# A decoder layer with 32 experts: ten chunks of expert weights ahead of the first expert, and another order of the x2 updates

## Chip, cores and metric

One core of a Trainium2 chip runs the kernel as one program. The metric is the device time in microseconds of an execution; 1505.49 us is the median of three (1504.41 to 1506.1).

## What is computed

The reference is one decoder layer on 256 tokens of 2048 columns in float32. `w_ada` times silu(c) gives six rows of 2048 (shift, scale and gate of both halves). The first half is a norm with shift and scale, one input projection, two token mixers (a gated linear recurrence, `hgrn`, and latent attention, `mla`) and one output projection, gated by `g1`. The second is a mixture of 32 experts of which each token takes two.

```python
h = _modulate(_rmsnorm(x, norm1_g[l]), sh1, sc1)
proj = h @ w_in[l]
...
mix = jnp.concatenate([o_a, o_b], axis=-1) @ w_out[l]
x = x + g1[:, None, :] * mix
h2 = _modulate(_rmsnorm(x, norm2_g[l]), sh2, sc2)
y = _hier_moe(h2, w_group[l], b_group[l], w_router[l], b_router[l],
              w_gate[l], w_up[l], w_down[l])
x = x + g2[:, None, :] * y
```

Inside `_hier_moe`: the softmax over four groups, the best group, the best two of its eight experts, and for each expert `(silu(xb @ w_gate) * (xb @ w_up)) @ w_down`, weighted and summed per token.

## The kernel before, in words

All weights come through one ring of buffers of [128, 4096] float32, 2048 KB a chunk, in one order (`items`): `w_ada`, `w_in`, the low-rank weights of the attention, `w_out`, then for each expert four chunks `gu` (gate and up) and two chunks `dn` (down). `ring_fill` (L156) issues the next load on SP's queue whenever a slot is free and `ring_done` (L172) frees a slot. Four slots are there from the start (`ringA`); two more (`ringB`, `RING2`) come when the temporaries of the mixers are closed behind `w_out(0, 1)` (`close_temps`, L794); and one (`ringC`) when the split buffers are closed behind the last dense product. So at most seven chunks of experts are in SBUF when the router ends. SP also loads x again, in tiles of 512 columns, for the residual (L556).

`dense` (L377) splits each 128 x 512 piece of weights in two parts: ScalarE rounds it (L385), VectorE takes the difference (L386), and TensorE makes three products with the split input (L400 to L402 here). `w_out(half, j)` runs the output projection for block j of 512 columns: half 0 over the attention's half of the rows into `mix0`, half 1 over the recurrence's. Behind half 1, three pairs of VectorE instructions (one for each 128 tokens) make the new residual (L549 to L551):

```python
V.tensor_add(m[:, t], m[:, t], ps[t])
V.tensor_mul(m[:, t], m[:, t], gate[:, 512 * j:512 * j + 512])
V.tensor_add(x2[j][:, t], x2[j][:, t], m[:, t])
```

`x2_ready` (L588) takes the squares of block j, transposes it on TensorE (`px2T`, L599), copies the transpose (L601, L603) and adds its part of the router's logits (`plog`, L607). The text calls block j of x2 a tile. Between the dense products TensorE computes the rows of `w_ada` (`pada`, L265); the last 24 of these matmuls belong to the gate of the second half, and `ada_end` adds them to a row `brows` (L274). `gate_rows` (L912) spreads that row over the partitions.

The router (L837 to L903) is a chain of small VectorE steps from the logits `lg` (L842) to the ranks of the tokens within their experts. `dispatch` (L919 to L944) gathers the tokens of four experts by matmuls with one-hot rows (`pgat`, L933) and evacuates with shift and scale (`XT`, L938). The expert loop then runs `pgu` (L1003), `hidden` and `down` (L979), and `combine` (L956).

Within an engine the instructions run in the order that the scheduler of the tile framework chose when the program was built; the Python text gives only priorities. SP issues its loads in the order of the text, and a load that waits holds all behind it.

Of the kernel before, what the change touches and what calls it, by code (L numbers as in the profile page):

```python
# [9 lines left out]
F32 = mybir.dt.float32  # L10
# [9 lines left out]
# buffers: weight ring, 4 KB tiles that live long, 4 and 2 KB temporaries, splits, more ring later  # L20
RING, NARENA, NTEMP, NSPLIT, RING2 = 4, 14, (8, 6), 4, 2
# rows of w_ada for the gates and the second modulation: chunks behind each step of the products
SPREAD = (1, 4, 7, 5, 5, 2, 0, 0, 0, 2, 1, 1, 0)
EARLY = {28: 1}
HEAD = 2  # expert chunks loaded ahead of the last of these rows
AHEAD = 3  # steps of the first dispatch ahead of the first expert
# [19 lines left out]
def tile_hybrid_layer(ctx, tc, A, out):  # L46
# [56 lines left out]
    # ---------------------------------------------------------------- weight stream  # L103
# [92 lines left out]
    # ---------------------------------------------------------------- start: x, tables  # L196
# [18 lines left out]
    # silu(c), by channel and as a row on every partition  # L215
# [14 lines left out]
    rows = cpool.tile([P, 512], F32, name="rows")  # L230
# [5 lines left out]
    def adt_chunk(i):  # L236
        """Two tiles of 128 columns of w_ada, transposed, times silu(c)."""
# [32 lines left out]
    def ada_end(b):  # L270
        if b in ("g1", "g2"):
            brow = brows[:, ("g1", "g2").index(b)]
            for j in range(4):
                V.tensor_add(brow[32 * j:32 * j + 1], brow[32 * j:32 * j + 1], acc[b][32 * j:32 * j + 1])  # L274
# [5 lines left out]
        else:  # L280
            S.activation(rows, acc[b], AF.Copy)
# [10 lines left out]
    def norm1():  # L292
        """x * rsqrt(mean(x^2) + eps)"""
# [871 lines left out]
```

## Time and profile before

| | |
|---|---|
| runs | 1504.41, 1505.49, 1506.1 us |
| profiled execution, span | 1503.6 us |
| PE, VectorE (DVE), ScalarE (ACT) busy | 75%, 39%, 23% |
| bytes moved, mean rate | 575.61 MB, 383 GB/s |
| rate in slices 17 to 39 of 40 | 428 to 431 GB/s |
| loads of expert chunks | 128 `gu` and 64 `dn`, 2048 KB each |

The page of the profile knows no time of the profiled execution but its span. Its other parts are read so: a group of instructions gives busy time, mean, and the idle time in front of it with what ended that; a window gives each engine's busy time in a stretch, PE's granted clock (1.00 is 2.4 GHz) and the DMA's share and rate; the timeline gives single instructions, or runs of like ones, with their start.

### The profile page before, as it was taken

How to read it: one execution, taken by the hardware profiler on the slowest of the kernel's cores; microseconds unless marked ns; L12 is line 12 of the kernel's file. 1: busy time of each engine (PE TensorE's matmuls, PEld its weight loads, DVE VectorE, ACT ScalarE, POOL GpSimd, SP SyncE). 2: the span in 40 equal slices, each digit the busy share in tenths (PEclk: the TensorE clock that was granted, in tenths of full speed). 3: DMA queues.
4: the chain of work that ended last, by engine and by line, in shares of the span. 5: the costliest groups of instructions: out<-in, count | busy, mean ns of one | idle time of the engine just before them, and what ended most of it. 6: DMA issues, size and time to landing. Idle time of an engine off the chain costs nothing. (4 is left out here: it accounts for less than half of the span.)

```text
span 1503.6 us, 22669 instructions
## 1 busy us (share of the span) xinstructions
PE 1123.6 (75%) x9813; PEld 686.8 (46%) x9813; DVE 592.3 (39%) x1192; ACT 340.5 (23%) x705; POOL 5.0 (0%) x9
## 2 busy tenths in 40 slices
PE   3799999979999989776667667657667657566555
PEld 1688887637568756333323323323423423333222
DVE  6789998759765552220121121113112112112112
ACT  4564446526435432100100100100100100000000
POOL 0000000000000000000000000000000000000000
PEclk9999999989999999878887888879978888889777
DMA  9788796877979798999999999999999999999995
GB/s 382 314 320 324 284 363 244 332 283 314 367 285 382 295 374 333 429 429 431 430 431 430 429 429 430 430 431 431 430 430 429 430 430 431 431 429 428 431 431 228
DMA packets 43423, 575.61 MB, mean 383 GB/s; under 512 B 4778, under 2 KB 5034, under 8 KB 8376
## 3 DMA queue, kind: packets, MB, share of 16 engines
q1 hardware_dynamic: 41776, 570.56, 91.2%
q10 hardware_dynamic: 1544, 3.56, 0.6%
q8 instruction: 79, 1.29, 0.3%
q14 instruction: 24, 0.20, 0.0%
HBM read 572.00 MB, written 2.11 MB: 382 GB/s over the span
## 5 line engine op out<-in xcount | busy, mean ns | idle before, releaser
L1003 PE MATMUL pgu<-wch,XT 128*32 128x256 f32 x4096 | 314.4, 461 | 188.5 <-DMA wch<-in_w_gu_dram 188.4
L1003 PEld LDWEIGHTS pgu<-wch,XT 128*32 128x32 f32 x4096 | 140.5, 127 | 353.7 <-DMA wch<-in_w_gu_dram 245.1
L979 PE MATMUL py<-wch,hT 128*32 128x256 f32 x2048 | 170.3, 490 | 80.3 <-DMA wch<-in_w_down_dram 73.5
L983 DVE TENSOR_TENSOR Y<-py,gate 32x256 f32<-32x256 f32 x256 | 107.6, 420 | 222.2 <-PE py L979 219.4
L968 DVE TENSOR_TENSOR hid<-sgu,pgu 128x128 f32<-128x128 f32 x32 | 9.2, 288 | 456.2 <-ACT sgu L966 456.2
L386 DVE TENSOR_TENSOR split<-wch,split 128x512 fp32r<-128x512 f32 (+2 forms) x248 | 160.2, 668 | 69.6 <-ACT split L385 68.4
L385 ACT ACTIVATE split<-wch 128x512 fp32r<-128x512 f32 (+2 forms) x248 | 148.1, 615 | 148.5 <-PE pacc L402 99.8
L979 PEld LDWEIGHTS py<-wch,hT 128*32 128x32 f32 x2048 | 80.1, 134 | 158.4 <-issue 63.1
L966 ACT ACTIVATE sgu<-pgu 128x128 f32<-128x128 f32 x32 | 8.9, 278 | 604.4 <-PE pgu L1003 604.4
L938 ACT ACTIVATE XT<-pgat,sh,a 128x128 f32<-128x128 f32 x128 | 48.2, 457 | 219.3 <-PE pgat L933 219.2
L401 PE MATMUL pacc<-split,hhi 128*128 128x512 f32 (+1 forms) x192 | 74.3, 387 | 2.3 <-DVE split L386 2.2
L393 PE MATMUL pacc<-hhi,split 128*128 128x256 f32 x256 | 72.7, 285 | 1.2 <-ACT split L385 1.1
L395 PE MATMUL pacc<-hhi,split 128*128 128x256 f32 x256 | 72.2, 285 | 1.7 <-DVE split L386 1.7
L402 PE MATMUL pacc<-split,hlo 128*128 128x512 f32 (+1 forms) x192 | 73.2, 382 | 0.0
L400 PE MATMUL pacc<-split,hhi 128*128 128x512 f32 (+1 forms) x192 | 71.1, 385 | 2.7 <-ACT split L385 2.7
L394 PE MATMUL pacc<-hlo,split 128*128 128x256 f32 x256 | 72.7, 285 | 0.5 <-DVE hlo L357 0.5
L243 DVE SCALAR_TENSOR_TENSOR wch<-wch,gate 128x2048 f32<-128x2048 f32 x32 | 72.8, 2285 | 0.0
L956 PE MATMUL pcmb<-Y,pwt 128*128 128x512 f32 x128 | 61.2, 622 | 15.5 <-DVE Y L983 15.5
L265 PE MATMUL pada<-wch,ca 128*1 128x512 f32 x512 | 69.9, 608 | 3.8 <-DVE pada L260 3.8
L933 PEld LDWEIGHTS pgat<-ohr,x 128*128 128x128 f32 x512 | 63.3, 205 | 10.4 <-issue 9.4
L933 PE MATMUL pgat<-ohr,x 128*128 128x128 f32 x512 | 66.7, 291 | 0.7 <-DVE sm L900 0.7
L400 PE MATMUL pacc<-split,mhi 128*128 128x512 f32 x128 | 51.0, 400 | 0.0
(301 smaller groups left out, 1187.7 us busy)
## 6 DMA issues: line engine op xcount, KB each, us to landing
wch<-in_w_gu_dram SPq DMA_DIRECT2D x128, 2048.0 KB, 31.1
wch<-in_w_down_dram SPq DMA_DIRECT2D x64, 2048.0 KB, 31.1
wch<-in_w_ada_dram SPq DMA_DIRECT2D x32, 2048.0 KB, 9.6
wch<-in_w_ada_t_dram SPq DMA_DIRECT2D x16, 2048.0 KB, 9.5
wch<-in_w_in_dram SPq DMA_DIRECT2D x16, 2048.0 KB, 9.3
wch<-in_w_out_dram SPq DMA_DIRECT2D x8, 2048.0 KB, 9.6
wch<-in_w_in_dram SPq DMA_DIRECT2D x4, 1664.0 KB, 7.5
x<-in_x_dram SPq DMA_DIRECT2D x8, 512.0 KB, 10.7
```

Source lines behind the costliest of these rows:

```text
L243: V.scalar_tensor_tensor(wk, wk, 1.0, gate, op0=OP.mult, op1=OP.mult, accum_out=r[:, k:k + 1])
L385: S.activation(s[:, 0, :ncol], w, AF.Copy)
L386: V.tensor_sub(s[:, 1, :ncol], w, s[:, 0, :ncol])
L393: PE.matmul(o, s[:, 0, c], hi, start=first and h % 2 == 0, stop=False, skip_group_check=True)
L394: PE.matmul(o, s[:, 0, c], lo, start=False, stop=False, skip_group_check=True)
L400: PE.matmul(o, hi[:, c], s[:, 0, :ncol], start=first, stop=False)
L401: PE.matmul(o, hi[:, c], s[:, 1, :ncol], start=False, stop=False)
L402: PE.matmul(o, lo[:, c], s[:, 0, :ncol], start=False, stop=stop)
L933: PE.matmul(ps[:, 128 * i:128 * i + 128], x2[kt // 4][:, t, 128 * (kt % 4):128 * (kt % 4) + 128], ohr[:, t], start=t == 0, stop=t == 1)
L979: PE.matmul(py[32 * j:32 * j + 32, :256], H["T"][:, 32 * kt:32 * kt + 32], w[:, 1024 * kt + 256 * j:1024 * kt + 256 * j + 256], start=kt = ...
L983: V.tensor_mul(Y[q][r:r + 32, 256 * j:256 * j + 256], py[32 * j:32 * j + 32, :256], gate[32 * j:32 * j + 32, c:c + 256])
L1003: PE.matmul(gu[32 * j:32 * j + 32, :256], XT[G4][kt // 8][:, kt % 8, 32 * e4:32 * e4 + 32], w[:, 1024 * i + 256 * j:1024 * i + 256 * j + 2 ...
```

## The change

It does these things:

- `RING2` is 3 instead of 2, so eight ring slots can hold chunks. The space comes from the constants (`cst` keeps 448 of its 1120 columns; the 672 that only the mixers need, `mst`, go to the temporaries and are loaded on ScalarE's queue), from `rows`, `rope`, `kr` and one of the two `brows`, and from single buffers in the pool `moe`.
- Two chunks, `gu` 3 of expert 0 and `gu` 0 of expert 1, are loaded into four free tiles each of the arena of 4 KB tiles (`LOANS`), by four loads of 512 KB, once the last dense product has been issued in the text.
- `w_out`: `mix0` is gated and added to x2 ahead of the dense product of half 1, so that behind it two pairs remain instead of three.
- The additions to `brow` get a lower priority (-150); the transposes of x2 go by token tile; half of the evacuations of the first `dispatch` go to VectorE.

The places in the order of the engines where this shows are these. In the names, `_` and numbers tell buffers apart.

The first is VectorE behind the recurrence of the second four heads (`hgrn(1)`), where the first output product `w_out(0, 0)` begins; `sm` are the steps of the normalisation, `o` its two products, `mlo` the evacuation of its transposes, `split` the pieces of `w_out`. Before:

```order
L446 TENSOR_SCALAR sm_624_3699<-sm_624_3699 128x8
L386 TENSOR_TENSOR split_641_3786<-wch_635_3752,split_641_3786 128x512
L386 TENSOR_TENSOR split_642_3795<-wch_635_3752,split_642_3795 128x512
L386 TENSOR_TENSOR split_643_3804<-wch_635_3752,split_643_3804 128x512
L190 TENSOR_TENSOR sm_629_3711<-sm_628_3709 128x8
L386 TENSOR_TENSOR split_644_3813<-wch_635_3752,split_644_3813 128x512
L191 TENSOR_TENSOR sm_629_3711<-sm_629_3711,sm_624_3699 128x8
L192 TENSOR_SCALAR sm_629_3711<-sm_629_3711 128x8
L386 TENSOR_TENSOR split_645_3822<-wch_635_3752,split_645_3822 128x512
L193 TENSOR_TENSOR sm_628_3709<-sm_628_3709,sm_629_3711 128x8
L523 TENSOR_TENSOR o_621_3674<-o_621_3674,sm_628_3709 128x1024
L386 TENSOR_TENSOR split_646_3831<-wch_635_3752,split_646_3831 128x512
```

Now:

```order
L471 TENSOR_REDUCE sm_625_3703<-sq_626_3704 128x4
L471 TENSOR_REDUCE sm_625_3703<-sq_627_3707 128x4
L472 TENSOR_SCALAR sm_625_3703<-sm_625_3703 128x8
L211 TENSOR_TENSOR sm_630_3715<-sm_629_3713 128x8
L212 TENSOR_TENSOR sm_630_3715<-sm_630_3715,sm_625_3703 128x8
L213 TENSOR_SCALAR sm_630_3715<-sm_630_3715 128x8
L214 TENSOR_TENSOR sm_629_3713<-sm_629_3713,sm_630_3715 128x8
L549 TENSOR_TENSOR o_622_3678<-o_622_3678,sm_629_3713 128x1024
L550 TENSOR_TENSOR o_622_3678<-o_622_3678,proj_94_578 128x1024
L463 SCALAR_TENSOR_TENSOR mlo_632_3723<-pmt_633_3724,pc_80,mhi_631_3722 128x4x128
L463 SCALAR_TENSOR_TENSOR mlo_632_3723<-pmt_634_3731,pc_80,mhi_631_3722 128x4x128
L412 TENSOR_TENSOR split_642_3790<-wch_636_3756,split_642_3790 128x512
```

The splits, which stood among the steps and products, stand behind `mlo`; ScalarE's half of the splits has moved behind its two `mhi` in the same way.

The second is VectorE from the end of the dense products to the router; `brow` is the row of the gate, `lg` the logits. Before:

```order
L603 COPY x2T_767_4625<-px2T_769_4632 128x512
L190 TENSOR_TENSOR sm_775_4661<-sm_774_4659 128x2
L191 TENSOR_TENSOR sm_775_4661<-sm_775_4661,sm_772_4654 128x2
L192 TENSOR_SCALAR sm_775_4661<-sm_775_4661 128x2
L193 TENSOR_TENSOR sm_774_4659<-sm_774_4659,sm_775_4661 128x2
L842 SCALAR_TENSOR_TENSOR lg_776_4666<-plog_698_4171,sm_774_4659,rb_3909 128x36 x2
L274 TENSOR_TENSOR brows_9_101<-brows_9_101,pada_658_3911 1x512
L847 TENSOR_REDUCE mx_777_4669<-lg_776_4666 128x2
L274 TENSOR_TENSOR brows_9_101<-brows_9_101,pada_658_3911 1x512
```

Now:

```order
L627 COPY x2T_752_4516<-px2T_754_4518 128x512
L299 TENSOR_TENSOR brow2_102<-brow2_102,pada_660_3916 1x512 x4
L584 TENSOR_TENSOR x2_757_4549<-x2_757_4549,mix0_699_4170 128x512 x2
L575 TENSOR_TENSOR mix0_699_4170<-pacc_758_4555,gate_85 128x512
L575 TENSOR_TENSOR mix0_699_4170<-pacc_759_4556,gate_85 128x512
L576 TENSOR_TENSOR x2_757_4549<-x2_757_4549,mix0_699_4170 128x512 x2
L627 COPY x2T_770_4637<-px2T_772_4639 128x512
```

The four additions (`x4`, L299 now) stood between steps of the router and stand ahead of the chain of x2 tile 3, which was ahead of them.

The same place on TensorE: the end of `w_out(1, 3)`, `pada`, transposes and logits. Before:

```order
L402 MATMUL pacc_756_4542<-split_764_4606,mlo_631_3719 128x512
L265 MATMUL pada_658_3911<-wch_735_4418,ca_109 1x512 x8
L265 MATMUL pada_658_3911<-wch_752_4527,ca_109 1x512 x8
L265 MATMUL pada_658_3911<-wch_753_4537,ca_109 1x512
L599 MATMUL px2T_768_4626<-cst_78,x2_754_4539 128x128
L599 MATMUL px2T_769_4632<-cst_78,x2_754_4539 128x128
L599 MATMUL px2T_768_4626<-cst_78,x2_754_4539 128x128 x3
L599 MATMUL px2T_769_4632<-cst_78,x2_754_4539 128x128 x3
L265 MATMUL pada_658_3911<-wch_753_4537,ca_109 1x512 x4
L607 MATMUL plog_698_4171<-wr2_655_3884,x2T_767_4625 128x128 x8
L265 MATMUL pada_658_3911<-wch_753_4537,ca_109 1x512 x3
L912 MATMUL pg2_817_4910<-brows_9_101,cst_78 128x512
```

Now (here the first row is the last of the dense product):

```order
L428 MATMUL pacc_759_4556<-split_767_4620,mlo_632_3723 128x512
L289 MATMUL pada_660_3916<-wch_737_4416,ca_111 1x512
L625 MATMUL px2T_753_4517<-cst_78,x2_739_4428 128x128 x2
L625 MATMUL px2T_754_4518<-cst_78,x2_739_4428 128x128 x2
L625 MATMUL px2T_753_4517<-cst_78,x2_739_4428 128x128 x2
L625 MATMUL px2T_754_4518<-cst_78,x2_739_4428 128x128 x2
L289 MATMUL pada_660_3916<-wch_737_4416,ca_111 1x512 x4
L631 MATMUL plog_701_4175<-wr2_657_3889,x2T_752_4516 128x128 x8
L289 MATMUL pada_660_3916<-wch_737_4416,ca_111 1x512 x3
L289 MATMUL pada_660_3916<-wch_738_4426,ca_111 1x512 x8
L289 MATMUL pada_660_3916<-wch_755_4537,ca_111 1x512 x8
L936 MATMUL pg2_827_4939<-brow2_102,cst_78 128x512
```

Transposes and logits of tile 2, which were inside the last dense product, are behind it; all `pada` and the gate's rows (`pg`) are ahead of tile 3's transposes.

The third is SP's queue there. Before:

```order
L556 DMA x2_736_4420<-in_x_dram 128x2x512
L163 DMA wch_752_4527<-in_w_ada_dram 128x4096
L163 DMA wch_753_4537<-in_w_ada_dram 128x4096
L556 DMA x2_754_4539<-in_x_dram 128x2x512
L163 DMA wch_770_4646<-in_w_gu_dram 128x4096
L163 DMA wch_771_4652<-in_w_gu_dram 128x4096
L163 DMA wch_797_4744<-in_w_down_dram 128x4096
L163 DMA wch_798_4754<-in_w_down_dram 128x4096
L163 DMA wch_799_4764<-in_w_gu_dram 128x4096
L163 DMA wch_809_4823<-in_w_gu_dram 128x4096
```

Now:

```order
L581 DMA x2_739_4428<-in_x_dram 128x2x512
L183 DMA wch_755_4537<-in_w_ada_dram 128x4096
L183 DMA wch_756_4547<-in_w_gu_dram 128x4096
L581 DMA x2_757_4549<-in_x_dram 128x2x512
L183 DMA wch_777_4673<-in_w_down_dram 128x4096
L172 DMA loan_773_4665<-in_w_gu_dram 128x1024
...
L183 DMA wch_778_4675<-in_w_down_dram 128x4096
L172 DMA loan_779_4677<-in_w_gu_dram 128x1024
L172 DMA loan_780_4678<-in_w_gu_dram 128x1024
```

The loads of tile 2 and of the last chunk of `w_ada` (the last `in_w_ada_dram` of each) have come closer to the end, and the eight loads `loan` stand ahead of the last chunks.

The diff, with comments and what the text above names in full left out:

```diff
-RING, NARENA, NTEMP, NSPLIT, RING2 = 4, 14, (8, 6), 4, 2
+RING, NARENA, NTEMP, NSPLIT, RING2 = 4, 14, (8, 6), 4, 3
+LOANS = (("gu", 0, 3), ("gu", 1, 0))
...
-C_ID, C_TRI64, C_ONE, C_TRI, C_MASK, C_IOTA, C_IOTM, C_FREQ, C_RESET = (
-    0, 128, 256, 384, 512, 768, 800, 832, 864)
-C_W = 1120
+C_ID, C_ONE, C_TRI, C_IOTA, C_IOTM = 0, 128, 256, 384, 416
+C_W = 448
+
+M_TRI64, M_MASK, M_FREQ, M_RESET = 0, 128, 384, 416
+M_W = 672
...
     cst = cpool.tile([P, C_W], F32, name="cst")
+    mst = temps.tile([P, M_W], F32, tag="mst", name="mst")
...
-    ring = {"next": 0, "cap": [[ringA, RING, 0]], "tile": {}, "limit": len(items)}
+    ring = {"next": 0, "cap": [[ringA, RING, 0]], "tile": {}, "limit": len(items), "loans": False}
+
+    def wcols(w, c, n):
+
+        return w[c // 1024][:, c % 1024:c % 1024 + n] if isinstance(w, list) else w[:, c:c + n]
 
     def ring_fill():
         while ring["next"] < ring["limit"]:
+            it = items[ring["next"]]
+            if it in LOANS:
+                if not ring["loans"]:
+                    return
+                src, _ = source(it)
+                t = [big([P, 1024], "loan") for _ in range(4)]
+                for i in range(4):
+                    nc.sync.dma_start(t[i], src[:, 1024 * i:1024 * i + 1024])
+                ring["tile"][ring["next"]] = (t, None)
+                ring["next"] += 1
+                continue
...
-        slot[2] -= 1
+        if slot is not None:
+            slot[2] -= 1
         ring_fill()
...
-    brows = big([P, 2, 512], "brows")
-    nc.scalar.dma_start(brows[0:128:32], A["b_g"].rearrange("b (j c) -> j b c", j=4))
+    brows = {"g2": cpool.tile([P, 512], F32, name="brow2")}
+    nc.scalar.dma_start(brows["g2"][0:128:32], A["b_g"][1].rearrange("(j c) -> j c", j=4))
     nc.sync.dma_start(cst, A["cst"])
+    S.dma_start(mst, A["mst"])
...
+        if ch == 0 and b == "g1":
+            brows[b] = tmp([P, 512], "brow1")
+            nc.scalar.dma_start(brows[b][0:128:32], A["b_g"][0].rearrange("(j c) -> j c", j=4))
...
-            brow = brows[:, ("g1", "g2").index(b)]
-            for j in range(4):
-                V.tensor_add(brow[32 * j:32 * j + 1], brow[32 * j:32 * j + 1], acc[b][32 * j:32 * j + 1])
+            brow = brows[b]
+            with tc.high_priority(-150 if b == "g2" else 0):
+                for j in range(4):
+                    V.tensor_add(brow[32 * j:32 * j + 1], brow[32 * j:32 * j + 1], acc[b][32 * j:32 * j + 1])
             if b == "g2":
                 return
...
+            rows = tmp([P, 512], "rows")
+    rope = temps.tile([P, 2, 2, 32], F32, tag="rope", name="rope")
+        kr = temps.tile([P, 2, 64], F32, tag="kr", name="kr")
...
-                V.tensor_add(m[:, t], m[:, t], ps[t])
-                V.tensor_mul(m[:, t], m[:, t], gate[:, 512 * j:512 * j + 512])
+                V.tensor_mul(m[:, t], ps[t], gate[:, 512 * j:512 * j + 512])
                 V.tensor_add(x2[j][:, t], x2[j][:, t], m[:, t])
             x2_ready(j)
 
         if half:
             x2[j] = big([P, 2, 512], "x2")
             nc.sync.dma_start(x2[j], A["x"][:, :, 512 * j:512 * j + 512])
+            for t in range(2):
+                V.tensor_mul(mix0[j][:, t], mix0[j][:, t], gate[:, 512 * j:512 * j + 512])
+                V.tensor_add(x2[j][:, t], x2[j][:, t], mix0[j][:, t])
...
-        for r in range(2):
-            ps = pm("px2T")
-            for i in range(2):
-                for t in range(2):
-                    c = 256 * i + 128 * t
-                    d0 = 128 * (2 * r + i)
-                    PE.transpose(ps[:, c:c + 128], x2[j][:, t, d0:d0 + 128], ident)
-            if r == 0:
-                S.activation(xT[:, 0:2], ps, AF.Copy)
-            else:
-                V.tensor_copy(xT[:, 2:4], ps)
+        px = [pm("px2T") for _ in range(2)]
+        for t in range(2):
+            for i in range(4):
+                c = 256 * (i % 2) + 128 * t
+                PE.transpose(px[i // 2][:, c:c + 128], x2[j][:, t, 128 * i:128 * i + 128], ident)
+        S.activation(xT[:, 0:2], px[0], AF.Copy)
+        V.tensor_copy(xT[:, 2:4], px[1])
...
-        nonlocal moe
         tmp_stack.close()
         ringB = late.enter_context(tc.tile_pool(name="ringB", bufs=RING2))
-        moe = late.enter_context(tc.tile_pool(name="moe", bufs=2))
...
+    moe = late.enter_context(tc.tile_pool(name="moe", bufs=2, side="right"))
     ring["cap"].append([ringC, 1, 0])
+    ring["loans"] = True
...
+                if G4 == 0 and i % 2:
+                    V.tensor_scalar(dst, src, a2[:, kt:kt + 1], sh2[:, kt:kt + 1], op0=OP.mult, op1=OP.add)
+                else:
+                    S.activation(dst, src, AF.Identity, bias=sh2[:, kt:kt + 1], scale=a2[:, kt:kt + 1])
...
-                              w[:, 1024 * i + 256 * j:1024 * i + 256 * j + 256], start=kt == 0, stop=kt == 15)
+                              wcols(w, 1024 * i + 256 * j, 256), start=kt == 0, stop=kt == 15)
```

## Rows read from the trace of the kernel before

**Rows 1.** The page's costliest groups: the first product of the experts.

```profile
L1003 PE MATMUL pgu<-wch,XT 128*32 128x256 f32 x4096 | 314.4, 461 | 188.5 <-DMA wch<-in_w_gu_dram 188.4
```

**Rows 2.** Windows: length, busy us (instructions) by engine, PEclk, DMA share, GB/s.

```profile
450.00:550.00 100.00, 99.95 (x513) 72.89 (x506) 54.66 (x84) 42.52 (x76) 0.00 (x0) 1.00 0.87 341
...
565.00:570.00 5.00, 3.51 (x16) 3.25 (x17) 2.67 (x16) 0.00 (x0) 0.00 (x0) 0.50 0.57 242
570.00:575.00 5.00, 5.00 (x56) 3.95 (x56) 0.00 (x0) 3.01 (x8) 0.00 (x0) 0.90 0.02 3
575.00:580.00 5.00, 5.00 (x61) 3.95 (x60) 0.00 (x0) 1.50 (x4) 0.00 (x0) 1.00 0.91 315
700.00:1400.00 700.00, 460.77 (x5071) 230.62 (x5070) 126.92 (x286) 48.95 (x143) 0.00 (x0) 0.84 1.01 430
```

**Rows 3.** Timeline of SP's queue: start, first to last issue's end, instruction, count.

```profile
527.01 5.47 SPq L163 DMA_DIRECT2D wch<-in_w_ada_dram  x2
...
555.80 22.94 SPq L163 DMA_DIRECT2D wch<-in_w_gu_dram  x3
...
574.56 0.33 SPq L163 DMA_DIRECT2D wch<-in_w_gu_dram  x1
```

**Rows 4.** Timeline, from the last dense matmul to the first expert product.

```profile
546.04 0.39 PE L402 MATMUL pacc<-split,mlo 128*128 128x512 f32 x1
...
547.07 1.29 DVE L550 TENSOR_TENSOR mix<-mix,gate 128x512 f32<-128x512 f32 x2
...
550.74 1.09 PE L599 MATMUL px2T<-cst,x 128*128 128x128 f32 x8
...
551.87 0.69 DVE L603 COPY x2T<-px2T 128x512 f32<-128x512 f32 x1 [1.15 <-PE px2T L599]
...
552.73 2.05 PE L607 MATMUL plog<-wr,x2T 128*128 128x128 f32 x16
...
554.82 0.42 DVE L842 SCALAR_TENSOR_TENSOR lg<-plog,sm,rb 128x36 f32<-128x36 f32 x2 [1.51 <-PE plog L607]
...
555.80 0.68 DVE L274 TENSOR_TENSOR brows<-brows,pada 1x512 f32<-1x512 f32 x1 [0.56 <-PE pada L265]
...
556.53 3.74 PE L912 MATMUL pg<-brows,cst 1*128 1x512 f32 x8 [0.79 <-DVE brows L274]
...
566.86 5.78 PE L933 MATMUL pgat<-ohr,x 128*128 128x128 f32 x32 [0.66 <-DVE sm L900]
...
572.57 1.93 PE L1003 MATMUL pgu<-wch,XT 128*32 128x256 f32 x32
```

**Rows 5.** Timeline around the start of the first output product.

```profile
429.39 3.61 PE L265 MATMUL pada<-wch,ca 128*1 128x512 f32 x30
...
430.82 0.69 DVE L445 TENSOR_REDUCE sm<-sq 128x4 f32<-128x512 f32 x1 [2.50 <-ACT sq L444]
...
432.93 0.50 PE L400 MATMUL pacc<-split,mhi 128*128 128x512 f32 x1
...
433.51 0.68 DVE L386 TENSOR_TENSOR split<-wch,split 128x512 fp32r<-128x512 f32 x1
...
436.09 1.23 DVE L523 TENSOR_TENSOR o<-o,sm 128x1024 f32<-128x1024 f32 x1
...
437.84 1.22 DVE L524 TENSOR_TENSOR o<-o,proj 128x1024 f32<-128x1024 f32 x1
...
439.20 1.06 PE L530 MATMUL pmt<-cst,o 128*128 128x128 f32 x8
...
439.87 0.69 ACT L436 ACTIVATE mhi<-pmt,pc 128x512 fp32r<-128x512 f32 x1 [0.41 <-PE pmt L530]
```

**Rows 6.** The page's DMA issues: count, KB each, median us from issue to landing.

```profile
wch<-in_w_gu_dram SPq DMA_DIRECT2D x128, 2048.0 KB, 31.1
...
wch<-in_w_ada_dram SPq DMA_DIRECT2D x32, 2048.0 KB, 9.6
...
x<-in_x_dram SPq DMA_DIRECT2D x8, 512.0 KB, 10.7
```

More of the change, by code (lines that the diff above doesn't have):

```diff
@@ L95, in tile_hybrid_layer @@
     ones = cst[:, C_ONE:C_ONE + 128]
-    tri64 = cst[:, C_TRI64:C_TRI64 + 128]
-    reset = cst[:, C_RESET:C_RESET + 256]
+    tri64 = mst[:, M_TRI64:M_TRI64 + 128]
+    reset = mst[:, M_RESET:M_RESET + 256]
     tri = cst[:, C_TRI:C_TRI + 128]
-    mask2 = cst[:, C_MASK:C_MASK + 256]
+    mask2 = mst[:, M_MASK:M_MASK + 256]
     iota = cst[:, C_IOTA:C_IOTA + 32]
@@ L229, in tile_hybrid_layer @@
     acc = {}
-    rows = cpool.tile([P, 512], F32, name="rows")
     sh1 = cpool.tile([P, 16], F32, name="sh1")
@@ L308, in tile_hybrid_layer @@
     posf = sm(2)
-    rope = cpool.tile([P, 2, 2, 32], F32, name="rope")
+    rope = temps.tile([P, 2, 2, 32], F32, tag="rope", name="rope")
     cos, sin = rope[:, 0], rope[:, 1]
@@ L315, in rotary @@
         for t in range(2):
-            V.tensor_scalar(ang[:, 32 * t:32 * t + 32], cst[:, C_FREQ:C_FREQ + 32], posf[:, t:t + 1], None, op0=OP.mult)
+            V.tensor_scalar(ang[:, 32 * t:32 * t + 32], mst[:, M_FREQ:M_FREQ + 32], posf[:, t:t + 1], None, op0=OP.mult)
         TWO_PI = 2.0 * np.pi
@@ L645, in mla_pre @@
             V.tensor_sub(kvT[:, 1, :, c], f, kvT[:, 0, :, c])
-        kr = cpool.tile([P, 2, 64], F32, name="kr")
+        kr = temps.tile([P, 2, 64], F32, tag="kr", name="kr")
         kg = tmp([P, 2, 64], "kg")
@@ L911, in gate_rows @@
             ps = pw("pg2")
-            PE.matmul(ps, ones[32 * j:32 * j + 1, :], brows[32 * j:32 * j + 1, 1], start=True, stop=True, tile_position=(32 * j, 0))
+            PE.matmul(ps, ones[32 * j:32 * j + 1, :], brows["g2"][32 * j:32 * j + 1], start=True, stop=True, tile_position=(32 * j, 0))
             S.activation(gate[:, 512 * j:512 * j + 512], ps, AF.Copy)
     def dispatch(G4):
-        oh = moe.tile([P, 2, 4, SL], F32, tag="oh", bufs=2, name=nm("oh"))
+        oh = moe.tile([P, 2, 4, SL], F32, tag="oh", bufs=1, name=nm("oh"))
         es = slice(4 * G4, 4 * G4 + 4)
@@ L937, in dispatch @@
                 dst, src = xt[kt // 8][:, kt % 8], ps[:, 128 * i:128 * i + 128]
-                S.activation(dst, src, AF.Identity, bias=sh2[:, kt:kt + 1], scale=a2[:, kt:kt + 1])
+                if G4 == 0 and i % 2:
+                    V.tensor_scalar(dst, src, a2[:, kt:kt + 1], sh2[:, kt:kt + 1], op0=OP.mult, op1=OP.add)
+                else:
+                    S.activation(dst, src, AF.Identity, bias=sh2[:, kt:kt + 1], scale=a2[:, kt:kt + 1])
             yield
@@ L964, in hidden @@
     def hidden(gu):
-        sg = moe.tile([P, 128], F32, tag="sg", bufs=2, name=nm("sgu"))
+        sg = moe.tile([P, 128], F32, tag="sg", bufs=1, name=nm("sgu"))
         S.activation(sg, gu[:, 0:128], AF.Silu)
-        hid = moe.tile([P, 128], F32, tag="hid", bufs=2, name=nm("hid"))
+        hid = moe.tile([P, 128], F32, tag="hid", bufs=1, name=nm("hid"))
         V.tensor_mul(hid, sg, gu[:, 128:256])
@@ L1077, in _consts @@
 def _consts():
-    c = np.zeros((P, C_W), np.float32)
+    c, m = np.zeros((P, C_W), np.float32), np.zeros((P, M_W), np.float32)
     i = np.arange(128)
@@ L1082, in _consts @@
     c[:, C_ID:C_ID + 128] = np.eye(128)
-    c[:, C_TRI64:C_TRI64 + 128] = same * (s <= t)
+    m[:, M_TRI64:M_TRI64 + 128] = same * (s <= t)
     c[:, C_ONE:C_ONE + 128] = 1.0
     c[:, C_TRI:C_TRI + 128] = s < t
-    c[:, C_MASK + 128:C_MASK + 256] = np.where(t <= s, 0.0, NEG)
+    m[:, M_MASK + 128:M_MASK + 256] = np.where(t <= s, 0.0, NEG)
     c[:, C_IOTA:C_IOTA + 32] = np.arange(32)
     c[:, C_IOTM:C_IOTM + 32] = np.arange(32) - 100.0
-    c[:, C_RESET:C_RESET + 256] = np.arange(256) % 64 != 0
-    c[:, C_FREQ:C_FREQ + 32] = (np.float32(10000.0) ** (-np.arange(0, 64, 2, dtype=np.float32) / np.float32(64))).astype(np.float32)
-    return c
+    m[:, M_RESET:M_RESET + 256] = np.arange(256) % 64 != 0
+    m[:, M_FREQ:M_FREQ + 32] = (np.float32(10000.0) ** (-np.arange(0, 64, 2, dtype=np.float32) / np.float32(64))).astype(np.float32)
+    return c, m
 def _layout(i):
@@ L1097, in _layout @@
     L = {}
-    L["cst"] = _consts()
+    L["cst"], L["mst"] = _consts()
     L["x"] = ac(np.asarray(i["x"])[0].reshape(2, P, D).transpose(1, 0, 2))
```

## The prediction

> **What bounds the kernel now.** I read the views from coarse to fine. The costliest groups come first: the first product of the experts (`pgu`) is 314.4 us of PE work, and in front of it PE idles for 188.5 us, nearly all of it waiting for a chunk of `w_gu` [rows 1]. The table of windows says the same of the memory side: from 700 to 1400 us the DMA moves 430 GB/s at a share of 1.01, while PE is busy for 460.77 of 700 us [rows 2]. So the expert part is a stream. A chunk of 2048 KB (2.097 MB) takes 2.097 / 430 = 4.87 us, and the end of the kernel is the time at which the stream starts for good, plus 4.87 us for each chunk that is still missing. Ahead of it lies the opposite: from 450 to 550 us PE is busy 99.95 of 100 us [rows 2], so there each microsecond added to PE's path moves everything behind it.
>
> Between the two lies the router, and there both starve. In 565 to 570 us the DMA moves 242 GB/s for 5 us, which is 2.8 us at 430, so the seventh chunk has landed at about 567.8. In 570 to 575 it moves 3 GB/s. In 575 to 580 it moves 315 GB/s, 3.7 us at 430, so it starts again at about 576.3 [rows 2]. **The hole is 8.5 us.** SP shows why: the seventh chunk is issued at 555.80, and the next at 574.56, when the first product of expert 0 has freed a slot [rows 3]. From issue to moving bytes, 576.3 - 574.56 = 1.8 us.
>
> **The change, part by part.**
>
> *Three more chunks.* If all ten are in when the first slot comes free, three fewer remain: 3 x 4.87 = 14.6 us gained, less whatever the release itself moves. With seven, expert work is not starved ahead of the release, so the release is the only clock that counts. I therefore follow the 574.56.
>
> *Router.* Before, the last product ends at 546.04 + 0.39 = 546.4, and the logits start at 554.82, 8.4 us later [rows 4]. In the new order PE runs 1 row product of `w_ada` (`pada`), the transposes of x2 tile 2 (1.09), 4 `pada`, the router product of tile 2 (2.05), then 19 `pada`. One costs 3.61 / 15 = 0.24 us [rows 5], each matmul being two records, so the last ends 1.09 + 2.05 + 24 x 0.24 = 8.9 us behind the dense end. The four `brow` additions wait for it (4 x 0.68 = 2.7), and VectorE runs in order, so the chain of x2 tile 3, though its product was ready at the dense end, starts only at 11.6. Its three pairs take 3 x 1.29 = 3.9 (15.5), transposes of the last half 0.55, copy 0.69, router product 2.05 [rows 4]: logits at 18.8. **The logits come 10.4 us later, counted from the dense end.** The shorter chain (one pair, 1.3 us, less behind the product) gains nothing there, since the chain is behind the additions. What comes back: before, the additions lie among the router's small steps, from 555.80 on, and logits to gather takes 566.86 - 554.82 = 12.0 us [rows 4]; without them I take off 3.2, the four additions and the gaps that they leave. A bound is 0 to 4. The gate's rows (3.74) now lie on PE while VectorE runs tile 3's chain, so they are hidden; uncovered they cost 3.7. From the gather to the first expert product nothing gets shorter: 572.57 - 566.86 = 5.7 on PE [rows 4]. Splitting the evacuation between ScalarE and VectorE helps only what PE does not itself hold up: nothing taken. Sum here: +10.4 - 3.2 = +7.2.
>
> *The dense end.* The transposes and router product of tile 2 (1.09 + 2.05 = 3.1) moved behind it: -3.1. The chains of tiles 0 and 1 now stand among the weight splits of the product after next, and PE's next step waits for them. The order puts six additions of 0.65 us, 3.9 us, in front of the next splits; the splits ahead cover part. I take 0.9 and 2.7, together +3.6, with 0 to 6 as bounds: before, such chains cost PE nothing that shows in 99.95 of 100 us [rows 2].
>
> *Start of the output product.* Before, four of its splits run among the small steps of the recurrence's normalisation, and its first matmul starts at 432.93 [rows 5]. Now all eight stand behind that chain on VectorE and ScalarE. Followed from the reduction at 430.82: 0.7, some 1.5 of small steps, the two products of 1.23 and 1.22, half of the transposes (0.5), two `mhi` of 0.69 and a split of 0.68 [rows 5] give about 438.0. That is +5.1, less the 1.06 of transposes that no longer interrupt the product. Nine `pada` moved from before this point to it, where they fill the wait; the place that they left is mostly bound by VectorE, and I take 1.0 of their 9 x 0.24 = 2.2. So +3.0, bounds +1 and +6.
>
> Release: +7.2 - 3.1 + 3.6 + 3.0 = **+10.7**. Against 14.6 that leaves **-3.9**. A second count goes by the hole: SP holds the second piece of the last borrowed chunk, and three chunks behind it, until x2 tile 3 is complete, 15.5 behind a dense end that is now 546.4 + 3.5 = 549.9, so at 565.4, moving at 567.2. The 6.25 chunks ahead, had they the old start, would be in 0.75 x 4.87 = 3.7 us before 567.8, at 564.1. The hole shrinks from 8.5 to 3.1: -5.4. I take -4.3 between the two. The profiled execution's span is 1503.6, 1.9 under the median of 1505.49; so 1499.3 on that scale, **1501.2 us on the median's**.
>
> The ring's third late slot, the split constants and the moved small pools cost nothing that I can find: the loads of constants are at the start, under product work. The borrowed chunks come as eight loads of 512 KB. The nearest row, x in 512 KB pieces, has 10.7 us from issue to landing beside 9.6 for 2048 KB of `w_ada` [rows 6]; both stand in a shared queue, so size alone decides little: nothing taken. If instead every piece paid 1.8 us of start by itself, 8 x 1.8 = 14.4 us would be lost, and the time would be 1515.6. That is a rival with little in its favour, since loads in this queue overlap: a chunk of `w_gu` has 31.1 us from issue to landing [rows 6] and yet one lands every 4.87. I give it 0.03. The Trainium skill (DMA: Bandwidth & Descriptors, Rules for kernel authors) asks for at least 1 MiB per DMA, and so speaks against these pieces. By the fit on that page for a DMA by itself (Anatomy of one DMA: 2.0 us and the bytes at 436 GB/s), as an estimate, eight pieces in turn would take 8 x 3.2 = 25.6 us in place of 9.7, and the time would be 1517. No row of this trace shows whether pieces in a queue pay that.
>
> **The rivals.** *The delays are hidden* (0.17). If VectorE's waits overlap better than the order suggests, the release moves by 3 us or so and the hole closes: -8.5 by the hole alone, up to -14.6 + 3 = -11.6. Time 1494 to 1497. For it: the small steps around 555 to 560 already run in the shadow of others. Against it: VectorE and PE are in order, and the `brow` additions wait on a definite matmul.
>
> *The last chunk of `w_ada` comes late* (slower, 0.10). Before, SP issued the last two by 532.5, 14 us ahead of the dense end [rows 3]. Now the last stands behind the load of x2 tile 2, which waits for the sum of tile 1, inside the last product: about 7 us ahead of the dense end. With 1.8 of start, 0.5 MB of x2 and its own 4.87 it lands about 1 us behind the dense end; it is needed at 7. Six us of slack decide it: each further microsecond delays additions, x2 tile 3, logits and the second half of the borrowing alike. 6 + 3.9 = 10 us late and nothing is left; a whole queue ahead of it, three chunks or 14.6 us, gives +4.7: 1510.
>
> *The ten are not there* (no measurable change, 0.20). SP's wait for tile 3 also lasts longer if the dense end is later. With the upper bounds (stalls 6, start +6) the release moves 16.1 and the hole remains: gain from 0 to 3, 1502.5 to 1505.5.
>
> **How the numbers follow.** The forecast has 0.50, and its own range is -8.5 to -0.5: 1497 to 1505. 0.2%, 3.0 us, is about what a measurement can tell. Of the forecast's chance, 0.42 lies beyond 3.0 and 0.08 within. With the first rival (0.17) and some of the third's (0.03), faster is 0.62; with the rest of the third's 0.17 same is 0.25; slower is 0.13 by the second rival and the 512 KB pieces. The range takes in most of the first rival and the third, 1494.0 to 1506.0.
>
> **What would show it.** Right: ten loads issued before the first wait for `pgu`; `brow` additions ahead of x2 tile 3's chain; logits 18 to 19 us behind the last dense matmul; the output product starting at 437 to 439; release near 585; a remaining DMA hole of 2 to 4 us before it. The forecast is wrong if logits come within 12 us of the dense end (first rival), if `pada` waits for its chunk (second), or if the DMA, once it restarts, runs below 430 GB/s or with gaps.

## The result, and the profile after

The changed kernel is slower: 1513.79 us (median of 4, 1510.97 to 1514.61) against 1504.95 us (median of 4), a ratio of 1.0056 with a 95% interval of 1.0044 to 1.0068: 0.6%, small but beyond the noise. The profiled execution's span is 1511.9 us, 8.3 above 1503.6. The forecast was 1501.2 us with a range from 1494.0 to 1506.0.

The new hole of the DMA at the router is small, as forecast: from 570 to 575 us 337 GB/s lack 1.1 us against 427, but at a share of 0.97, so the engines are not idle there; they move the second half of the borrowed pieces. Windows of the kernel after (columns as in rows 2):

```profile
390.00:400.00 10.00, 9.09 (x48) 7.22 (x47) 7.59 (x14) 5.53 (x11) 0.00 (x0) 0.93 0.00 0
...
570.00:575.00 5.00, 3.33 (x20) 2.74 (x18) 2.81 (x15) 1.06 (x4) 0.00 (x0) 0.77 0.97 337
...
585.00:590.00 5.00, 5.00 (x55) 3.63 (x55) 1.58 (x4) 1.72 (x4) 0.00 (x0) 0.91 1.01 429
590.00:600.00 10.00, 9.81 (x130) 6.55 (x129) 3.30 (x9) 3.24 (x6) 0.00 (x0) 1.00 0.97 373
...
700.00:1400.00 700.00, 456.31 (x5056) 229.35 (x5047) 126.25 (x281) 48.93 (x142) 0.00 (x0) 0.84 1.01 427
```

Two rows there were not expected. From 390 to 400 us the DMA moves nothing at all. And the stream of the experts runs at **427 GB/s where it ran at 430** [rows 2], at the same share of 1.01: the engines are as busy and move less.

The timeline of the kernel after, from the first output product (`pacc`) to the gather (to be read against rows 4 and 5):

```profile
440.96 0.50 PE L426 MATMUL pacc<-split,mhi 128*128 128x512 f32 x1
...
552.77 0.40 PE L428 MATMUL pacc<-split,mlo 128*128 128x512 f32 x1
...
558.02 4.46 PE L289 MATMUL pada<-wch,ca 128*1 128x512 f32 x38
...
562.54 2.83 DVE L299 TENSOR_TENSOR brow<-brow,pada 1x512 f32<-1x512 f32 x4 [6.68 <-PE pada L289]
...
565.40 1.29 DVE L584 TENSOR_TENSOR x<-x,mix 128x512 f32<-128x512 f32 x2
...
568.72 1.94 PE L625 MATMUL px2T<-cst,x 128*128 128x128 f32 x8 [0.85 <-PE pg L936]
...
570.91 2.68 PE L631 MATMUL plog<-wr,x2T 128*128 128x128 f32 x16 [0.26 <-ACT x2T L626]
...
573.63 0.42 DVE L866 SCALAR_TENSOR_TENSOR lg<-plog,sm,rb 128x36 f32<-128x36 f32 x2 [0.72 <-PE plog L631]
...
582.43 5.47 PE L957 MATMUL pgat<-ohr,x 128*128 128x128 f32 x32 [0.66 <-DVE sm L924]
```

and SP's queue:

```profile
558.17 12.35 SPq L172 DMA_DIRECT2D loan<-in_w_gu_dram  x4
570.62 2.35 SPq L183 DMA_DIRECT2D wch<-in_w_gu_dram  x3
589.94 4.17 SPq L183 DMA_DIRECT2D wch<-in_w_down_dram  x2
```

VectorE idles 6.68 us until the last `pada` is done, takes the four additions, and only then starts x2 tile 3. The first slot comes free at 589.94, where it was 574.56 [rows 3]: +15.4. Three chunks are worth -14.6, which leaves +0.8. The bytes in the trace agree: from 600 us on the kernel after has 0.17 chunks more to load than the kernel before, 0.8 us. (In 590 to 600 us its DMA lacks 1.3 us, 373 of 427, but the kernel before also waited, 1.8 us, behind its own release.) The 182 chunks still to come cost 2.097 MB / 427.0 - 2.097 / 429.9 = 0.033 us each, +6.1 (the rates to a tenth are the loads' packets of 16 KB counted in the trace from 700 to 1400 us of its own clock, which starts 11 us ahead of the span: 18242 after, 18365 before). Together +6.9 of the 8.3. The other 1.4 us arise behind 1400 us, and no run explains them.

So two questions stand: why is the stream slower, and why did the release move by 15.4 us instead of 10.7?

### The profile page after: what moved, and what is told of

It reads as the page before. It is cut to its first block, busy times and chain, and to the rows that moved or that the text cites. A ratio compares the mean times of both kernels' runs of the same rounds, so it can differ in the third digit from the quotient of the medians.

```text
span 1511.9 us, 22674 instructions
## 1 busy us (share of the span) xinstructions
PE 1117.5 (74%) x9813; PEld 685.6 (45%) x9813; DVE 602.3 (40%) x1208; ACT 338.1 (22%) x697; POOL 5.0 (0%) x9
## 4 chain that ended last, share of the span: by engine, by line
DMA 54%; PE 34%; DVE 8%; ACT 2%; issue 1%; SPq 0%; ACTq 0%
DMA wch<-in_w_gu_dram 38%; DMA wch<-in_w_down_dram 15%; PE pacc L427 5%; PE pacc L428 5%; PE pacc L426 5%; PE pgu L1030 4%; PE pada L289 3%; PE py L1006 2%; DVE wch L264 2%; PE pacc L421 1%; PE pacc L419 1%; PE pgat L957 1%; PE pacc L420 1%; DVE split L412 1%; DVE proj L450 1%
## 5 line engine op out<-in xcount | busy, mean ns | idle before, releaser
L1030 PE MATMUL pgu<-wch,XT 128*32 128x256 f32 x4032 | 308.5, 460 | 194.9 <-DMA wch<-in_w_gu_dram 194.9
L1006 PE MATMUL py<-wch,hT 128*32 128x256 f32 x2048 | 163.6, 475 | 79.1 <-DMA wch<-in_w_down_dram 75.6
```

Source lines behind the costliest of these rows:

```text
L1006: PE.matmul(py[32 * j:32 * j + 32, :256], H["T"][:, 32 * kt:32 * kt + 32], w[:, 1024 * kt + 256 * j:1024 * kt + 256 * j + 256], start=kt = ...
L1030: PE.matmul(gu[32 * j:32 * j + 32, :256], XT[G4][kt // 8][:, kt % 8, 32 * e4:32 * e4 + 32], wcols(w, 1024 * i + 256 * j, 256), start=kt == ...
```

## The stream at 427 GB/s

Seven of the eight slots of the ring start, within a partition, at odd multiples of 128 bytes in the changed kernel (33920, 50304, and so on), since the smaller constants moved all that lies behind them; before, six of seven started at odd multiples of 256 (37632, 54016). The last slot, on the right of SBUF, starts at 212960 in both, off a multiple of 256 too. Theory A: this start sets the rate. Theory B: eight queued chunks instead of seven do. Theory C: where the inputs lie in HBM.

**e1**, one slot less:

```diff
-RING, NARENA, NTEMP, NSPLIT, RING2 = 4, 14, (8, 6), 4, 3
+RING, NARENA, NTEMP, NSPLIT, RING2 = 4, 14, (8, 6), 4, 2
```

> The changed kernel with RING2 back at 2: seven slots and the two borrowed chunks, nine chunks in all. The chunks start at the same addresses as in the changed kernel. The changed kernel streams experts at 427 GB/s, the kernel before at 430. Theory A (the start of a chunk within its partition, an odd multiple of 128 bytes in the changed kernel, an even one before): still 427 GB/s between 700 and 1400 us, and one chunk less, about +5 us: 1518. Theory B (eight chunks queued instead of seven): back at 430, so +5 - 6: 1512 to 1513. Theory C (where the inputs lie in HBM): 427, 1518.

Measured: 1512.48 us (1.005, 1.0034 to 1.0067), the stream at 427:

```profile
700.00:1400.00 700.00, 454.94 (x5040) 229.24 (x5028) 126.44 (x282) 49.39 (x144) 0.00 (x0) 0.84 1.01 427
```

The rate speaks against B. The time alone would have spoken for it, and by an accident: with another order of the scheduler the gate's additions fell behind x2 tile 3, and the logits came at 564.3 instead of 573.6, which paid for the missing chunk.

**e2** moves the changed kernel's tiles by 128 bytes, **e3** those of the kernel before:

```diff
-    pc = cpool.tile([P, P_W], F32, name="pc")
+    pcw = cpool.tile([P, P_W + 32], F32, name="pc")
+    pc = pcw[:, 0:P_W]
```

> The changed kernel with 128 unused bytes ahead of the weight ring in each partition, so that seven of the eight slots start at a multiple of 256 bytes, as six of seven did before. Theory A: 430 GB/s between 700 and 1400 us and about 6 us less, 1507 to 1508. Theories B and C: 427 GB/s and 1513 to 1514, no change.

> The kernel before with the same 128 unused bytes, so that its slots start at odd multiples of 128 bytes. Theory A: 427 GB/s between 700 and 1400 us and about 6 us more, 1511. Theories B and C: 430 GB/s and 1505, no change.

Measured: e2 1506.59 us (1.0006, 0.9997 to 1.0016), e3 1512.42 (1.0051, 1.0035 to 1.0068). The window from 700 to 1400 us, of e2 and of e3:

```profile
700.00:1400.00 700.00, 454.11 (x5068) 229.26 (x5072) 128.13 (x286) 49.48 (x144) 0.00 (x0) 0.85 1.01 430
```

```profile
700.00:1400.00 700.00, 451.70 (x5041) 227.56 (x5043) 125.19 (x281) 49.48 (x144) 0.00 (x0) 0.85 1.01 427
```

128 unused bytes in a kernel make 7 us either way. Theory A is shown as far as the address goes, B and C fall: the kernel before has seven slots and its own inputs, and runs at 427 once it is moved. Which address, and what boundary, took more runs.

**e10** and **e11** are e3 with 64 and with 256 bytes (`P_W + 16`, `P_W + 64`), one run each:

> The kernel before with 64 unused bytes ahead of the ring: slots start at multiples of 64 bytes, not of 128. Theory (a multiple of 256 bytes is what counts): as with 128 bytes, 427 GB/s between 700 and 1400 us, 1511 to 1513. Rival (smaller offsets cost in proportion, or finer ones more): between 427 and 430, or below 427.

> The kernel before with 256 unused bytes ahead of the ring: slots start at multiples of 512 bytes, where they started at odd multiples of 256. Theory: 430 GB/s between 700 and 1400 us and 1505, no change. Rival (the boundary that counts is 512 bytes or more, and the kernel before had only part of it): above 430 GB/s.

Measured: e10 1513.68 us and 427 GB/s, e11 1503.91 us and 430:

```profile
700.00:1400.00 700.00, 457.75 (x5048) 230.31 (x5040) 125.21 (x281) 49.47 (x144) 0.00 (x0) 0.84 1.01 427
```

```profile
700.00:1400.00 700.00, 452.60 (x5052) 226.75 (x5044) 128.59 (x289) 47.34 (x139) 0.00 (x0) 0.85 1.01 430
```

Off a multiple of 256 bytes, 64 cost as much as 128; an odd multiple of 256 costs nothing beside a multiple of 512.

**e9** is e6 (below) with the slot on the right of SBUF, the only one still off, moved to a multiple of 256:

```diff
+    edge = late.enter_context(tc.tile_pool(name="edge", bufs=1, side="right")).tile([P, 56], F32, name="edge")
+    V.memset(edge[0:1, 0:1], 0.0)
     ringC = late.enter_context(tc.tile_pool(name="ringC", bufs=1, side="right"))
```

> The run with the late gate row, and 224 unused bytes ahead of the eighth slot, the only one that still starts off a multiple of 256 bytes (212960, now 212736). Theory (each load pays for its own start): one load in eight gets 0.7% faster, the stream rises from 429.9 to about 430.3 GB/s between 700 and 1400 us, and the time falls by 0.7 us, less than a comparison can tell: 1494 to 1496. Rival (one slot off the multiple costs nothing, what matters is something that seven slots share): 429.9 GB/s.

Measured: 1496.13 us and 18371 packets, beside 18368 in e6; one load in eight would have been worth some 15 packets. The theory that each load pays for its own start misses here. **e13 to e15** take the kernel before and shift a part, one run each: e13 the four early slots (128 bytes ahead of them and, in a pool `edge`, 128 behind), e14 the arena and the two late slots (the 128 behind only), e15 the slot on the right by 96 bytes.

> The kernel before with 128 unused bytes ahead of the four early slots and 128 behind them: these four start at odd multiples of 128 bytes, the arena and the two late slots at multiples of 256. Theory 1 (each load pays for its own start; moving six slots cost 2.9 GB/s, 0.48 a slot): 427.9 GB/s between 700 and 1400 us. Theory 2 (it is not the chunks but the tiles of the arena, which moved with them): 429.9. Theory 3 (a few slow loads set the pace of all): 427.0.

> The kernel before with 128 unused bytes behind the four early slots: arena and the two late slots start at odd multiples of 128 bytes, the four early ones at multiples of 256. Theory 1: 428.9 GB/s. Theory 2: 427.0. Theory 3: 427.0.

> The kernel before with 96 unused bytes ahead of the seventh slot alone, which starts at an odd multiple of 128 bytes (212864) instead of 212960. Theory 1, with any start off a multiple of 256 bytes paying the same: 429.9 GB/s, as before, since it is off in both. Theory 1, with the start at 212960 paying nothing for a reason of its own: 429.4. Theory 2: 429.9. Theory 3: 427.0 if this slot counts like the others.

By the packets of 16 KB between 700 and 1400 us of the trace's clock:

```
kernel                       slots off 256   packets   GB/s
e9                                0 of 8      18371    430.0
before, e15                       1 of 7      18365, 18366   429.9
e14 (and all of the arena)        3 of 7      18358    429.7
e13                               5 of 7      18308    428.5
e3, e1                            7 of 7      18242, 18245   427.0
after                             8 of 8      18242    427.0
```

None of the three theories has its numbers in all three runs. That the arena's tiles alone do it falls (e14 moves them all and loses 0.2 GB/s). If it is the chunks, it is not slot by slot: the loss grows faster than the share of slots that are off, and one or three of seven cost next to nothing. But e3, e10 and e13 also move the constants behind `pc` and the small tiles, which e14 and e15 leave in place. No run moves the four early slots without these tiles, so a part of the loss may be theirs. Why the parts don't add up stays open.

## The router, and what the ten chunks are worth

**e4** gives one small tile back its own place:

```diff
-            rows = tmp([P, 512], "rows")
+            rows = temps.tile([P, 512], F32, tag="rows", name=nm("rows"))
```

> The changed kernel with the row `rows` in a tile of its own instead of one of the six 2 KB temporaries. Theory: in the changed kernel the copy into `rows` waits until the softmax gives a temporary back (399.9 us instead of 378.4), which stops the rows of w_ada and their loads, and moves the splits of the first output product behind the recurrence. Then here the copy stands at about 378, the first output product starts near 433 instead of 441, the dense end falls from 553 to about 546, and the time by 6 to 8 us: 1506 to 1508, the stream still at 427 GB/s. Rival: the wait comes from the constants on the other queue or the longer x2 chain; then the product still starts near 441 and the time stays at 1513.

Measured: 1505.52 us (1.0004, 0.9995 to 1.0014). The line of the copy into `rows` in the kernel before, after, and in e4 (first and last start at the end):

```profile
L281 ACT ACTIVATE rows<-pada x2: 597/597/597, 378.4 to 447.3; 128x512 f32<-128x512 f32 x2
```

```profile
L307 ACT ACTIVATE rows<-pada x2: 577/587/597, 399.9 to 454.7; 128x512 f32<-128x512 f32 x2
```

```profile
L307 ACT ACTIVATE rows<-pada x2: 597/597/597, 378.5 to 447.0; 128x512 f32<-128x512 f32 x2
390.00:400.00 10.00, 10.00 (x66) 8.74 (x65) 8.58 (x16) 8.13 (x14) 0.00 (x0) 1.00 0.77 329
...
432.67 0.49 PE L426 MATMUL pacc<-split,mhi 128*128 128x512 f32 x1
```

In the changed kernel `rows` is one of six temporaries of 2 KB that the softmax uses too. The copy out of `pada` therefore comes 21.5 us later, no further rows of `w_ada` can be multiplied until then, their chunks keep their slots, and the DMA has nothing to load from 390 to 400 us. PE, which filled the softmax's waits with these rows, is busy for 15.97 of 20 us from 380 to 400 instead of 20. With its own tile the first output product starts at 432.67, the dense products end at 545.5, and the time falls by 8.3 us. The rival (the constants, the x2 chain) is out.

**e5** has both repairs, e2's and e4's.

> The changed kernel with both repairs: the 128 unused bytes and `rows` in a tile of its own. Theory: the two causes are independent, so the gains add: stream at 430 GB/s, 6 to 7 us below the run with `rows` alone (1505.5): 1499, and 6 us below the kernel before. Rival: with the stream at 430 the chunks wait elsewhere (an earlier end of the stream uncovers the work behind it) and the sum of the two is not reached: 1502 to 1505.

Measured: 1499.08 us (0.9957, 0.9943 to 0.9971), 14.7 below the changed kernel; the two alone gave 7.2 and 8.3. They add up within 0.8 us.

**e6** also holds the gate's additions back, in place of the priority of -150:

```diff
+                if b == "g2":
+                    tc.add_manual_dep(add.ins, held[0].ins.name, ...)
...
+        held[G4] = V.tensor_mul(oh, oh, bc(W[:, :, es, None], [P, 2, 4, SL]))
...
+    side = dispatch(0)
+    next(side)
     for it in g2:
         ada_chunk(it[1], it[2])
-    side = dispatch(0)
-    for _ in range(AHEAD):
+    for _ in range(AHEAD - 1):
```

> As the run before, with the four additions of the gate's row held behind the one-hot rows of the first dispatch, so that VectorE takes x2 tile 3 first. Theory: the logits come some 13 us behind the last dense matmul instead of 21, the first slot is freed 8 us earlier; of that the time gets only what is left of the idle of the DMA after 550 us, some 4 to 10 us: 1490 to 1495. Rival: the DMA has no idle left to give and the release is no bound with ten chunks; then the time stays at 1499.

Measured: 1495.55 us (0.9937, 0.992 to 0.9953), 3.5 below e5, just short of the expected gain. The logits, the gather and the additions in e6, and its DMA:

```profile
556.81 0.42 DVE L869 SCALAR_TENSOR_TENSOR lg<-plog,sm,rb 128x36 f32<-128x36 f32 x2 [1.03 <-PE plog L634]
...
565.62 5.21 PE L960 MATMUL pgat<-ohr,x 128*128 128x128 f32 x32 [0.66 <-DVE sm L927]
566.17 2.82 DVE L299 TENSOR_TENSOR brow<-brow,pada 1x512 f32<-1x512 f32 x4
```

```profile
540.00:550.00 10.00, 10.00 (x63) 6.04 (x65) 6.80 (x12) 2.04 (x5) 0.00 (x0) 1.00 1.01 428
550.00:560.00 10.00, 6.31 (x54) 3.33 (x46) 5.44 (x25) 2.90 (x11) 0.00 (x0) 1.00 0.99 397
560.00:570.00 10.00, 6.21 (x34) 5.84 (x35) 7.31 (x30) 0.20 (x1) 0.00 (x0) 0.66 1.04 436
570.00:580.00 10.00, 7.91 (x72) 4.88 (x74) 1.52 (x4) 3.68 (x9) 0.00 (x0) 0.83 1.01 431
580.00:590.00 10.00, 9.28 (x136) 5.47 (x132) 3.59 (x10) 3.44 (x7) 0.00 (x0) 1.00 1.00 428
```

The logits come 12.9 us behind the end of the last dense matmul (543.9), and 9.9 earlier than in e5 (566.7). Only 3.5 of that reach the time, because the DMA now runs without a hole from 560 on: the release is no longer what bounds.

**e7** is e6 with `RING2` 2 and `LOANS` empty: seven chunks.

> As the run with the late gate row, but with two late ring slots and no borrowed chunks: seven chunks, all else as there. Theory (three chunks are worth what the hole of the DMA at the router is worth): the hole is back, about 8 us, and the time is 6 to 9 us above the run with ten chunks. Rival (the three chunks add nothing, because SP waits in front of them anyway): the same time as with ten, within 2 us.

Measured: 1501.73 us (0.9978, 0.9968 to 0.9987), 6.2 above e6. From 570 to 580 us its DMA moves

```profile
570.00:580.00 10.00, 10.00 (x135) 6.81 (x138) 2.59 (x8) 3.60 (x7) 0.00 (x0) 1.00 0.74 272
```

so the hole is back. Three chunks are worth 6.2 us here, not 14.6: they can give no more than the idle that they fill.

**e8** issues the loads of x2 and of the borrowed pieces from GpSimd (`nc.gpsimd.dma_start` instead of `nc.sync.dma_start`, in both places).

> As the run with the late gate row, but the loads of x2 and of the borrowed pieces are issued from GpSimd's queue, so that SP's queue is not held by their waits. Theory: the waits of SP for the sum of x2 tiles and for free arena tiles leave the DMA idle between 520 and 560 us (about 14 us in the run with `rows` alone); without them 5 to 10 us less than the run with the late gate row. Rival: those holes come from slots that are not yet free, which no queue changes: the same time within 2 us, or a little more because these loads are slower to issue.

Measured: 1501.34 us (0.9969, 0.996 to 0.9979), 5.8 above e6: neither theory. With the queue the order of VectorE changed too. The second load of x2, the addition that needs it and the splits beside it, and VectorE's waits for x2 from 480 to 560 us, first in e8:

```profile
499.50 0.73 POOL L584 DMA_DIRECT2D x<-in_x_dram  x1 [19.24 <-DVE x L579]
...
511.24 1.29 DVE L587 TENSOR_TENSOR x<-x,mix 128x512 f32<-128x512 f32 x2 [10.02 <-DMA x<-in_x_dram]
512.45 2.49 DVE L415 TENSOR_TENSOR split<-wch,split 128x512 fp32r<-128x512 f32 x4
...
DVE x L587 <- DMA x<-in_x_dram: 20.9, 3, 10.0
```

and in e6:

```profile
512.33 0.55 SPq L584 DMA_DIRECT2D x<-in_x_dram  x1
...
526.24 0.69 DVE L415 TENSOR_TENSOR split<-wch,split 128x512 fp32r<-128x512 f32 x1 [0.71 <-ACT split L414]
526.85 1.29 DVE L587 TENSOR_TENSOR x<-x,mix 128x512 f32<-128x512 f32 x2
...
DVE x L587 <- DMA x<-in_x_dram: 0.6, 1, 0.6
```

In e8 this load is issued 12.8 us earlier than in e6, and from issue to landing the four loads of x2 take about as long (median 10.1 us, 9.5 in e6). But the scheduler has put the addition in front of most splits of the dense product, where e6 has it behind them. So VectorE waits for the load, and the splits behind it wait too: 20.9 us in three waits, where it was 0.6. e8 changes queue and order together; what the queue alone is worth stays open.

**e12** is e6 with the old x2 chain (the three pairs of the kernel before; nothing ahead of the product).

> The run with the late gate row, with the x2 chain of the kernel before (three pairs behind the product, nothing ahead of it). Theory A (the shorter chain is worth its pair): logits 1.3 us later, but the release is no bound by then, so within 1.5 us of 1495.5, above it. Theory B (the pair ahead of the product makes VectorE wait for the load of x2 in front of the splits, and costs more than it gives): the dense end comes 2 to 4 us earlier, the holes of the DMA between 520 and 560 us shrink, and the time is 1492 to 1494.

Measured: 1498.55 us (0.9959, 0.9945 to 0.9973), five runs from 1495.91 to 1499.94. B's mechanism is there (the dense products end at 541.4 instead of 543.9) but not its gain, and A's bound is missed too. The profiled execution is the fastest of the five, so what costs the others 3 us isn't in its trace. That the shorter chain gains is likely by the medians, why is open.

## Why the prediction was wrong

Its outcome and sign failed, by two terms above all: the moved tiles, put at nothing, cost 6.1 us, and the start of the output product, put at +3.0, came at +8.0. Most of the other steps held. Added up, the release moved by 6.7 (dense end) + 12.1 (logits behind it) - 3.2 (logits to gather) - 0.3 (gather to first product) + 0.1 (first product to free slot) = 15.4, where +10.7 was forecast.

- **"cost nothing that I can find"**, of the moved constants and pools: the largest error, +6.1 us. The working priced instructions and loads and never asked where the smaller constants put the ring. No row of the trace before shows this, but the addresses were there to be compared.
- **Start of the output product**, "+3.0, bounds +1 and +6": the product starts 8.0 later. The order was read rightly, splits behind the recurrence. But "the place that they left is mostly bound by VectorE, and I take 1.0", a gain, was a loss: the last products of the recurrence (`po`) ended 2.5 us later, since PE lost 4 of the 20 us from 380 to 400 and the DMA stood still from 390 on (in e4 they end as early as before). I took the missing rows of `w_ada` as moved work and didn't ask what they waited for. The dense end came at +6.7 instead of +3.5; from the product's start to the dense end the kernel after is 1.3 us shorter, so the moved products and chains cost no more than was put down for them.
- **Logits**, 18.8 us behind the dense end: 20.5. The order was as described. Transposes and router product took 1.94 and 2.68 us instead of 1.09 and 2.05: the granted clock, 1.00 from 560 to 565 us, where PE was busy for 4.21 of 5 us, is 0.54 from 565 to 570 and 0.50, the 1.2 GHz level, while the transposes run (568.72 to 570.66). I had taken them at full rate, and only half of the transposes behind the chain.
- **"without them I take off 3.2"**: logits to gather takes 8.8 us, exactly that, and again in e6 (565.62 - 556.81). Gather to first product takes 5.4, forecast 5.7.
- **The hole**, "2 to 4 us": 1.1 in 570 to 575, where the engines are busy, and 1.3 in 590 to 600. The count by the release was the right one, and with 589.94 it makes three chunks worth nothing: +15.4 against -14.6. The count by the hole had the hole, but not its gain of 5.4: it took the chunks ahead to be where they were before, and at 565 us the trace has them 1.4 chunks, 6.9 us, behind.
- **Rivals.** Slower came true with 0.13, but not by its mechanism: the last chunk of `w_ada` is issued at 540.44 and `pada` runs without a wait from 558.02 on. The third rival, in which the delays eat the gain (0.20, no change, with a release up to 16.1 later), describes what the router did: with the addresses put right, e2 measures 1506.59, no change beyond the noise.
- **The pieces of 512 KB**, taken at nothing, do cost something: in e6 they move from 555.0 to 567.2 us, in packets of 4 KB, and the DMA moves 397 and 436 GB/s in the two windows from 550 to 570. Such a packet takes 165 ns on average in e6 and 175 in the kernel after, where a quarter of a 16 KB packet is 153 and 154; for 1024 packets on 16 engines that is 0.7 and 1.3 us, as an estimate. So the 0.03 for 14.4 us was right to be small, and the rule of the Trainium skill on 1 MiB per DMA (DMA: Bandwidth & Descriptors, Rules for kernel authors) has a small price here, where loads queue; whether it is the load's size or its rows of 4 KB no run separates. The fit that the prediction took from that page (Anatomy of one DMA) is stated there for DMAs that GpSimd issues, and these are SP's.
- The idea of the change holds: with two small repairs and the additions held back it is 0.6% faster than before (e6), 3 chunks giving 6.2 us of that.

## What to carry to other kernels

When a change resizes any tile, compare the start addresses of all streamed tiles before and after: the cost of a bad start sits in no instruction, only in the rate of a window at full DMA share. When a tile moves into a shared pool, list who holds that pool's buffers at the moment it is needed; a 2 KB copy that waits can stop a chain of loads and products. And a prefetch is worth the idle that it fills, so once the release stops being the bound, an earlier router buys nothing.

## What the runs showed of the hardware

A load of rows of 16 KB into SBUF is 0.7% slower if most of its buffers, and the small tiles that moved with them, start off a multiple of 256 bytes: 427.0 against 429.9 GB/s, by 64 or by 128 bytes alike (e3, e10), and nothing at an odd multiple of 256 (e11). The mean of a 16 KB packet goes from 612.9 to 616.8 ns. The Trainium skill (DMA: Bandwidth & Descriptors, How a descriptor splits into AXI transactions) says that a descriptor that starts off a 256-byte boundary pays for the bytes in front of it, 128 bytes being 4 of the 512 beats of a 16 KB row, 0.8% as an estimate. The page says it of what a transaction reads, and not of a destination in SBUF. The size agrees with e3; by that rule 64 bytes would cost half as much, which e10 contradicts, and each slot would pay for itself, which e9 and e13 to e15 do not bear out.
